# The stores' DMAs move from SyncE's queue to ScalarE's

## The chip, the cores and the metric

The kernel runs on one core of a Trainium2 chip. The metric is the device time of one execution in microseconds (us), the median of the runs shown. One execution was also taken with the hardware profiler; the rows below are of that one.

## The reference

The reference runs two blocks in a row on a sequence of 1024 tokens with 1024 features. The first block has two layers. Each layer mixes a grouped-query attention over the sequence and 256 context tokens, a windowed pooling and a neighbourhood attention on a grid of 64 columns; the context is updated in the first layer only.

```python
def first_block(x, c, ctx, ...):
    for l in range(2):
        h  = rms_norm(x, norm_gain[l]) * (1 + scale) + shift      # scale, shift, gate from silu(c) @ w_mod[l]
        hc = rms_norm(ctx, norm_gain[l]) * (1 + scale_c) + shift_c
        aq, ak, av, ag, bz, bg, nq, nk, nv, ng = split(h @ w_in[l])
        a_out = global_gqa(rope(norm(aq)), rope(norm(ak)), av, norm(ak_c), av_c)
        b_out = pool_branch(bz, pool_w[l], pool_scale[l])
        n_out = neighbourhood_attn(norm(nq), norm(nk), nv, norm(nk_c), nv_c, na_rpb[l])
        y = concat([a_out * silu(ag), b_out * silu(bg), n_out * silu(ng)]) @ w_out[l]
        x = x + gate * y
    return x

def second_block(x, p, ...):
    z = rmsnorm(x, g_mix) @ w_in
    y_fox  = fox_attention(q, k, v, log_f)               # causal, 8 heads, a decay as bias
    y_rwkv = rwkv7_scan(r, decay, k, v, -kk, kk * a)     # a recurrence over the 1024 tokens, 8 heads
    x = x + (sigmoid(gate_fox) * (y_fox @ w_o_fox) + sigmoid(gate_rwkv) * (y_rwkv @ w_o_rwkv)) @ w_out
    u = causal_dwconv(rmsnorm(x, g_ffn) @ w_up)
    x = x + (gelu(u[:, :2816]) * u[:, 2816:]) @ w_down
    return x + sigmoid(rmsnorm(x, g_ple) @ w_ple_gate) * (p @ w_ple_up)
```

## The kernel before

Activations lie with features on the 128 partitions and tokens along the free dimension. A product of full accuracy is made of three matmuls: each operand is split into a rounded part (`wh`, `h`; a cast on ScalarE, lines 271, 280 and 282) and the remainder (`wl`; a subtraction on VectorE, line 272). A weight tile comes by DMA into one of two raw buffers `wr` (line 290), is split, and the raw buffer is free again when the subtraction is done.

The stages follow each other in this order.

- **First block, twice** (`gqa`, `na`, `mix`). `gqa` projects queries, keys and values, takes the row maxima of the scores (`max_steps`) and then the exact softmax (`exact_steps`). One step of `exact_steps` makes, for each of two heads, a score bank `sp` on TensorE (two buffers) and its exponential `p` on ScalarE (line 694); the product with the values follows one step later. At the end of a pair of heads ScalarE copies the sum out (line 728), VectorE takes the reciprocal of the row sums (line 729), GpSimd multiplies (line 730), and the result `yr` is stored to the DRAM tensor `yd`. While the last attention units run, `na_project` makes the neighbourhood attention's queries, keys and values, 20 pieces of 128 tokens in each layer, and stores each piece to DRAM: `nv` to `nvd`, and the turned tiles `nt` to `nk1d`, `nk2d` and `nq1d` (lines 980 and 985). ScalarE or VectorE copies `nt` out of PSUM (lines 321 and 323). `na` loads them again, gates its result on GpSimd (line 1093) and stores it; beside it run the gates (`gate_steps`, a GpSimd product at line 950) and the pooling. `mix` loads all of `yd` (line 278, `h<-yd`) and the residual (line 1139, `x<-xd`), multiplies by `w_out` and adds in place (line 1148).
- **Second block**: `project` (projections, many stores of intermediates), `rwkv` (the recurrence as a chain of small matmuls with the causal attention woven in; its results are stored at line 1758 from `yc`, those of the attention from `yr`), `merge` (loads `yd` and, at line 1815, `x<-xd`), and `ffn` with 16 stores of the output at its end.

Every intermediate that goes through DRAM is written by one helper, `store` (lines 739 and 740). All loads, and the few stores that are not written with the helper, name SyncE's queue (SP) themselves.

What sets the order: the code is written in program order with two streams woven into each other (`weave`), but the framework's planner makes each engine's instruction stream from it. The planner keeps its own account of when operands and buffers are ready and puts the instruction that is ready and stands first in the program next. An engine, and the queue that it issues, then work strictly in that fixed order on the chip. An instruction waits for what it needs, and all that stands behind it on the same engine waits with it. A DMA instruction that SP issues thus stands in SP's stream, and one that ScalarE issues stands between ScalarE's activations and copies.

Of the kernel before, what the change touches and what calls it, by code (L numbers as in the profile page):

```python
# [216 lines left out]
class _Builder:  # L217
# [519 lines left out]
        return steps  # L737

    def store(self, dst, src):
        self.nc.sync.dma_start(out=dst, in_=src)  # L740

    def first_block(self):
        nc, tc, a = self.nc, self.tc, self.a
# [1212 lines left out]
```

## Time and profile before

| | |
|---|---|
| median of 3 runs | 4063.01 us (4056.43 to 4072.8) |
| profiled execution, its own time | 4071.35 us |
| its span, first to last instruction | 4069.6 us |
| mean granted TensorE clock | 0.955 |
| TensorE matmuls busy | 3755.1 us (92%) |
| VectorE / ScalarE / GpSimd busy | 2386.8 / 1612.1 / 929.7 us (59 / 40 / 23%) |
| DMA engines | 29.8% of 16 engines' span, all from one queue |

The profiled execution's own time is 1.75 us above its span and 8.3 us above the median of the runs. TensorE is the engine that the span follows; the rest of its time is spread over waits for other engines. DMA-issuing instructions are not counted as busy on any engine: on SP they are listed as SPq. A granted clock of 1.00 is full speed.

### The profile page before, as it was taken

Reading aid. Unit: us, or ns where it says so; the run is one execution under the profiler, and the core shown is the slowest. Engines: PE = TensorE matmul, PEld = TensorE weight load, DVE = VectorE, ACT = ScalarE, POOL = GpSimd, SP = SyncE. Lnnn points to the kernel's source line nnn. Section 1 sums busy time; section 2 is a strip of 40 time slices with the busy share of each in tenths; the row PEclk is TensorE's granted clock in tenths of the full one; section 3 lists DMA queues with packets and bytes.
Section 4 is the critical chain, followed back from the end, with each engine's and each line's share of the span. In section 5 each row is a group of like instructions: output and inputs, shape, how many; then the busy total and the mean of one; then the engine's idle time right before and its main releaser. Section 6 shows DMA issues by size and latency. Waiting matters only on the chain. (4 is left out here: it accounts for less than half of the span.)

```text
span 4069.6 us, 52648 instructions
## 1 busy us (share of the span) xinstructions
PE 3755.1 (92%) x18392; PEld 2809.5 (69%) x18392; DVE 2386.8 (59%) x5500; ACT 1612.1 (40%) x3251; POOL 929.7 (23%) x1127
## 2 busy tenths in 40 slices
PE   5899999888899999799999989989869999999999
PEld 4755666566755666478778866666648788888877
DVE  5888755645787747655664337776544543434354
ACT  4445663334346653543333234443343422222243
POOL 3233322311233324311110023343312100000020
PEclk8999999989999999899999978998879999999999
DMA  5111126564111135543333242121224411111133
GB/s 179 46 43 42 55 88 188 188 215 147 39 42 40 56 129 191 166 129 89 108 100 102 87 115 55 47 69 23 68 100 143 149 50 47 50 47 47 49 92 105
DMA packets 267890, 379.20 MB, mean 93 GB/s; under 512 B 56400, under 2 KB 145440, under 8 KB 264024
## 3 DMA queue, kind: packets, MB, share of 16 engines
q1 hardware_dynamic: 267624, 375.83, 29.8%
q8 instruction: 146, 2.39, 0.3%
q14 instruction: 120, 0.98, 0.1%
HBM read 280.90 MB, written 87.54 MB: 91 GB/s over the span
## 5 line engine op out<-in xcount | busy, mean ns | idle before, releaser
L223 PE MATMUL pp<-h,wh 128*128 128x512 f32 (+1 forms) x1696 | 527.3, 388 | 50.6 <-DVE x L1148 16.9
L223 PE MATMUL pp<-wh,h 128*128 128x384 f32 (+1 forms) x1792 | 518.2, 352 | 15.4 <-ACT v L548 12.6
L272 DVE TENSOR_TENSOR wl<-wr,wh 128x512 fp32r<-128x512 f32 (+3 forms) x386 | 299.7, 781 | 393.4 <-ACT wh L271 391.6
L223 PE MATMUL dd<-h,wh 128*128 128x512 f32 x1664 | 519.5, 393 | 0.0
L271 ACT CAST wh<-wr 128x512 fp32r<-128x512 f32 (+3 forms) x386 | 249.9, 651 | 611.3 <-PE pp L223 286.7
L223 PEld LDWEIGHTS pp<-h,wh 128*128 128x128 f32 x1696 | 315.7, 194 | 128.9 <-ACT wh L271 17.8
L709 POOL TENSOR_TENSOR acc<-acc,p 128x512 f32<-128x512 f32 (+3 forms) x246 | 295.3, 1200 | 443.3 <-ACT p L694 275.7
L223 PEld LDWEIGHTS dd<-h,wh 128*128 128x128 f32 x1664 | 312.5, 188 | 71.4 <-DVE h L478 0.3
L223 PEld LDWEIGHTS pp<-wh,h 128*128 128x128 f32 x1792 | 335.2, 194 | 34.0 <-ACT v L548 13.9
L223 PE MATMUL rp<-h,side 128*128 128x512 f32 x1440 | 350.6, 396 | 0.0
L223 PE MATMUL pp<-h,wl 128*128 128x512 f32 (+1 forms) x848 | 327.1, 386 | 1.0 <-DVE wl L272 0.9
L223 PE MATMUL dd<-h,wl 128*128 128x512 f32 x832 | 325.9, 392 | 0.0
L223 PE MATMUL pp<-wl,h 128*128 128x384 f32 (+1 forms) x896 | 312.6, 349 | 0.0
L223 PE MATMUL sp<-q,k 66*128 66x512 f32 (+6 forms) x944 | 300.1, 407 | 11.2 <-DVE p L692 5.7
L223 PEld LDWEIGHTS rp<-h,side 128*128 128x128 f32 x1440 | 266.5, 189 | 52.0
L634 DVE TENSOR_REDUCE mx<-mp 128x1 f32<-128x512 f32 (+1 forms) x472 | 250.7, 559 | 55.3 <-PE mp L223 53.4
L223 PE MATMUL mp<-k,q 128*128 128x512 f32 (+3 forms) x664 | 232.5, 383 | 13.5 <-DVE mx L634 6.4
L709 DVE TENSOR_TENSOR acc<-acc,p 128x512 f32<-128x512 f32 (+3 forms) x246 | 201.1, 817 | 68.0 <-ACT p L694 26.8
L223 PEld LDWEIGHTS sp<-q,k 128*128 128x128 f32 (+1 forms) x944 | 164.0, 192 | 108.7 <-issue 55.7
L694 ACT ACTIVATE p<-sp 128x512 f32<-128x512 f32 (+1 forms) x316 | 181.4, 594 | 141.3 <-PE sp L223 128.1
L223 PE MATMUL pp<-act,wh 128*128 128x512 f32 x704 | 221.4, 396 | 2.0 <-ACT act L271 1.1
L223 PE MATMUL vp<-p,v 128*64 128x512 f32 (+3 forms) x824 | 212.9, 596 | 5.5 <-ACT p L694 5.1
(371 smaller groups left out, 6705.5 us busy)
## 6 DMA issues: line engine op xcount, KB each, us to landing
wr<-in_w_out SPq DMA_DIRECT2D x96, 256.0 KB
wr<-in_w_up SPq DMA_DIRECT2D x88, 256.0 KB
wmod<-in_w_mod SPq DMA_DIRECT2D x16, 1024.0 KB
wr<-in_w_tok SPq DMA_DIRECT2D x40, 384.0 KB
xd<-x SPq DMA_DIRECT2D x6, 2048.0 KB
wr<-in_w_feat SPq DMA_DIRECT2D x40, 256.0 KB
bq<-in_na_bias SPq DMA_DIRECT2D x16, 640.0 KB
yd<-yr SPq DMA_DIRECT2D x32, 256.0 KB
```

The lines of the kernel that those rows point to most:

```text
L223: return self.nc.tensor.matmul(out, lhsT=lhsT, rhs=rhs, start=start, stop=stop)
L271: self.nc.scalar.copy(out=hi, in_=src)
L272: self.nc.vector.tensor_tensor(out=lo, in0=src, in1=hi.bitcast(F32), op=ALU.subtract)
L634: nc.vector.tensor_reduce(out=m, in_=ps[:, :n], axis=AX.X, op=ALU.max)
L694: made = nc.scalar.activation(out=p[:, j, :n], in_=st[:, :n], func=AF.Exp)
L709: u.summed = eng.tensor_tensor(out=u.acc[:, j, q0:q0 + n], in0=u.acc[:, j, q0:q0 + n], in1=p[:, j, :n], op=ALU.add)
```

## The change

The helper that writes every intermediate and the output issues its DMA on ScalarE's queue instead of SP's. All loads stay on SP, and so do the few transfers that do not go through the helper (queries from SBUF to SBUF, the two bounces of the recurrence through DRAM, and the row `crow`).

```diff
     def store(self, dst, src):
-        self.nc.sync.dma_start(out=dst, in_=src)
+        self.nc.scalar.dma_start(out=dst, in_=src)
```

## Rows read from the trace of the kernel before

**Rows 1.** The page: busy time, share of the span and instructions of each engine.
```profile
PE 3755.1 (92%) x18392; PEld 2809.5 (69%) x18392; DVE 2386.8 (59%) x5500; ACT 1612.1 (40%) x3251; POOL 929.7 (23%) x1127
```

**Rows 2.** Stretches: length, busy PE, PEld, DVE, ACT, POOL, clock, DMA share, GB/s.
```profile
350.00:600.00 250.00, 237.92 (x1148) 155.79 (x1147) 178.29 (x408) 153.27 (x325) 85.60 (x112) 1.00 0.19 55
...
1300.00:1500.00 200.00, 189.88 (x911) 127.98 (x911) 132.93 (x325) 130.09 (x271) 64.77 (x90) 1.00 0.21 63
...
1800.00:2400.00 600.00, 562.26 (x2765) 472.69 (x2765) 293.29 (x911) 188.29 (x481) 58.51 (x146) 0.97 0.34 104
```

**Rows 3.** Line 740, the store: count, issue in ns (least/median/most), first and last start.
```profile
L740 SPq DMA_DIRECT2D nvd<-nv x40: 327/331/566, 338.0 to 1482.8; - x40
L740 SPq DMA_DIRECT2D nk1d<-nt x40: 522/532/610, 370.3 to 1485.5; - x40
L740 SPq DMA_DIRECT2D nk2d<-nt x40: 838/857/928, 374.5 to 1486.7; - x40
...
L740 SPq DMA_DIRECT2D nq1d<-nt x36: 531/546/905, 375.5 to 1492.7; - x36
```

**Rows 4.** Waits of SP's queue: line, what it waited for, us in total, times, longest.
```profile
SPq L290 <- DVE wl L272: 1050.6, 303, 15.4
SPq L740 <- POOL yr L730: 136.4, 23, 23.4
...
SPq L740 <- DVE nt L323: 42.9, 24, 4.5
...
SPq L740 <- POOL yr L1093: 35.9, 9, 9.0
...
SPq L740 <- POOL kk L1406: 17.7, 7, 5.9
...
SPq L740 <- POOL gy L950: 15.3, 8, 4.2
```

**Rows 5.** Waits between TensorE and the exponentials, 350 to 600 us.
```profile
PEld vp L223 <- ACT p L694: 11.1, 30, 1.4
...
ACT p L694 <- PE sp L223: 26.2, 26, 2.0
```

**Rows 6.** Lines 729 and 730, between the copy of a result and its store.
```profile
L729 DVE RECIPROCAL yr<-sp x38: 1745/3358/3359, 165.1 to 2998.3; 128x512 f32<-128x512 f32 x32, 128x256 f32<-128x256 f32 x6
...
L730 POOL TENSOR_TENSOR yr<-yr x38: 727/1282/1722, 166.9 to 3001.8; 128x512 f32<-128x512 f32 x32, 128x256 f32<-128x256 f32 x6
```

**Rows 7.** Timeline around the end of `rwkv`: start, us, instruction [idle before <-releaser].
```profile
3003.11 0.33 SPq L740 DMA_DIRECT2D yd<-yr  x1
...
3008.44 0.32 SPq L740 DMA_DIRECT2D yd<-yc  x1
3008.85 0.39 SPq L1815 DMA_DIRECT2D x<-xd  x1
3010.70 0.37 SPq L278 DMA_DIRECT2D h<-yd  x1
...
3024.55 1.22 PE L223 MATMUL pp<-h,wh 128*128 128x512 f32 x2 [16.54 <-ACT wh L271]
```

**Rows 8.** Timeline at the end of the second `na`.
```profile
1665.09 29.87 SPq L290 DMA_DIRECT2D wr<-in_w_out  x5
1697.41 0.33 SPq L740 DMA_DIRECT2D yd<-yr  x1
...
1698.31 0.41 SPq L1139 DMA_DIRECT2D x<-xd  x1
...
1707.69 1.22 PE L223 MATMUL pp<-h,wh 128*128 128x512 f32 x2 [14.14 <-DVE x L1148]
```

**Rows 9.** Timeline inside `rwkv`, a result's store on SP and ScalarE's stream beside it.
```profile
2518.24 0.53 SPq L1322 DMA_DIRECT2D kk<-fk2d  x1
2528.70 0.34 SPq L740 DMA_DIRECT2D yd<-yr  x1
...
2527.22 0.58 ACT L1663 COPY tq<-c 128x512 f32<-128x512 f32 x1 [3.67 <-PE c L223]
```

## The prediction

> **What bounds the kernel now.** I read the page's busy line first. The reader is to see that TensorE's matmuls fill 92% of the span and ScalarE's own work only 40% [rows 1]: whatever costs TensorE no time costs nothing, and ScalarE has room on average. An average hides the stages, so the stretches come next [rows 2]. In the two stretches in which the softmax runs beside the neighbourhood projections (350 to 600 and 1300 to 1500 us) ScalarE is busy 153.27 of 250 and 130.09 of 200 us, 61% and 65%, and TensorE 95%. In `project` (1800 to 2400) ScalarE is busy 31%. Then the store line by itself, for what one issue holds a queue [rows 3], and the waits of SP's queue, for what stands ahead of what [rows 4]. The waits between TensorE and the exponentials tell how close these two engines run [rows 5]. Last come the timelines where TensorE stands longest, to see whether a load was late because a store stood ahead of it [rows 7, 8].
>
> **What the change removes from SP.** Nearly all loads of weights wait for their raw buffer, not for the queue: 1050.6 us of SP's waiting is for the subtraction that frees `wr` [rows 4]. Such a load does not start earlier when stores leave the queue. I cost this at nothing; the cover is that split weights lie several tiles ahead, and no wait of TensorE in the rows of the inner loops names a load.
>
> Stores do stand ahead of loads where a stage ends. At the end of `rwkv`, SP issues a store at 3003.11 and the next at 3008.44; the 2 MB residual load goes out at 3008.85, and the last load of `yd`, whose casts and products come last ahead of TensorE's first matmul after 16.54 us of idleness, only at 3010.70, behind those 2 MB [rows 7]. With the second store gone from SP the residual can go right after what is left of SP's work, at about 3005.6, so some 3.3 us earlier, and the last load of `yd` lands as much earlier. At the end of the second `na` SP is through with the loads ahead at 1694.96, then waits until 1697.41 for the store's operand, and issues the residual at 1698.31; TensorE waits 14.14 us for the chain behind it [rows 8]. Here the gain is 2.4 us. Together I take **6 us off**. Bounds: nothing, if the residual's buffer comes free no earlier than that; and 30.7 us, the two idle times whole, if it had been ready long before. I stay near the low end, because after the residual still come a load, two casts and a subtraction that do not change.
>
> By the Trainium skill, DMA: Bandwidth & Descriptors, section Issuing engines are not separate DMA queues, issuing from more than one engine saves only the sequencer's time for starting the DMA. By that rule the waiting ahead of these loads is no gain and the sum below would be 6 us higher; no row of the kernel before, where one queue issues all, decides it.
>
> **What it adds to ScalarE: the issues.** Of the stores of line 740 the four rows of the neighbourhood projections stand here; 15 more rows, 266 stores, are most of them like the row of `nvd` [rows 3]. Those of the projections hold a queue for 40 x 0.331 + 40 x 0.532 + 40 x 0.857 + 36 x 0.546 = 88.5 us, 156 instructions, nearly all inside the two stretches. There ScalarE goes from 283.4 to 371.9 of 450 us, from 63% to 83%, and each issue stands in order between the exponentials that TensorE waits for.
>
> How much of it reaches TensorE is read from the two sides of the softmax [rows 5]: TensorE's weight loads for the value products waited 30 times for an exponential, 0.37 us each, and ScalarE waited 26 times for the scores, 1.0 us each. So about half of the exponentials have no slack, the other half have about 1 us, which hides one issue. I charge half of the 156 stores with 0.37 us: **29 us**. Bounds: nothing, if the planner lays every issue into ScalarE's idle time; 88.5 us, if every one is passed on whole.
>
> The other stores have cover: over a third of them lie in `project`, where a bank of TensorE is filled by 24 matmuls and ScalarE is two thirds idle [rows 2]. I cost them at nothing; without that cover, at 0.33 us each, the 266 would be 88 us.
>
> **What it adds to ScalarE: the waits.** Where ScalarE itself made the operand, the store waits for work that ScalarE does anyway. Where GpSimd made it, ScalarE stands still until GpSimd is done, with every activation behind it. SP's waits for such operands are 136.4 + 35.9 + 17.7 + 15.3 = 205.3 us in 23 + 9 + 7 + 8 = 47 places [rows 4]. The longest chain is the one of a softmax result: after ScalarE's copy the reciprocal takes 3.36 us and GpSimd's product 1.28 us [rows 6]. One case stands in `rwkv` [rows 9]: SP has nothing to issue from 2518.77 to 2528.70; ScalarE stands idle for 3.67 us of it and has one copy at 2527.22 that TensorE's chain needs. A store that the planner puts ahead of this copy holds the chain for about 1.5 us, from 2527.22 to 2528.70; one that it puts behind, hardly.
>
> Since the planner goes by its own account, not by the chip, I take half of the 47 places as put too early, by one product of GpSimd, 1.28 us: **30 us**. Bounds: nothing, and all of the 205.3 us. I stay far below the upper end because SP waits with nothing else to do, while ScalarE reaches the same store later, with other work done ahead of it. Waits for VectorE's `nt` are 42.9 us on SP in 24 places [rows 4]; they fall on stores that are charged above, and I add nothing for them; 42.9 us is their bound.
>
> By the Trainium skill, Perfetto Trace Analysis, section Per-instruction lifecycle, an activation goes into a wait queue and leaves the sequencer free, while a DMA keeps the sequencer from its wait until its descriptors are made. By that rule these waits hold all of ScalarE's later work. No row of the kernel before shows a store in ScalarE's stream.
>
> For the clock I take nothing: the stretches with many short waits run at 1.00 [rows 2].
>
> **The sum.** 29 + 30 - 6 = 53 us on the profiled execution: its own time of 4071.35 becomes about 4124. That execution is 8.3 us above the median of the runs, 4063.01, so the forecast for a median is 4063 + 53 = **4116 us**. About 0.5% (20 us) is what a measurement of this kernel can tell from no change.
>
> **The rivals.**
>
> *ScalarE jams (slower than forecast).* If the planner's account of GpSimd and of the reciprocal is short in most places, the 205.3 us of waits move onto ScalarE, and the 88.5 us of issues pass on too. Half of the two, 147 us, gives 4210. For it: the three engines' chain is long [rows 6], and 83% in order leaves little room. Against it: outside the two stretches ScalarE is busy 1612.1 - 283.4 = 1328.7 of about 3620 us, 37% [rows 1, 2].
>
> *No change.* The planner sees ScalarE's idle 37% in the stretches and puts stores there and behind work that is ready. Charges of a third of mine, 20 us, less the 6 us, give 4077, within 20 us of before. For it: ScalarE's idle time before an exponential is 1.0 us and most issues are 0.33 to 0.55 us [rows 3, 5]. Against it: the issue of `nk2d`, 0.86 us, and the two beside it come within a few us of each other in each piece.
>
> *Faster.* The loads at the ends of the stages are what counts. If the residual loads were ready 10 us or more before SP came to them, each of the two idle times [rows 7, 8] shrinks by that, some 22 us together, the charges on ScalarE stay in its idle time, and the time is 4041. It decides from about 10 us of earlier issue at each; the case for it is that SP did stand waiting for a store in both places, the case against it that only 3.3 and 2.4 us of that waiting is seen right ahead of the residuals.
>
> *The change does not do what it says:* the planner could order the rest of SP's stream so that loads wait as before, which is again no change in time; it is in that rival's chance.
>
> **How the numbers follow.** The forecast, slower by 20 to 100 us, has 0.50; the jam, above 100 us, 0.17; no change 0.22; faster by over 20 us 0.11. Slower by over 0.5% is then 0.50 + 0.17 = 0.67. The range: below 4042 lies about half of the faster case, 0.06; above 4200 a good half of the jam, 0.10. So 4042 to 4200 holds the time in about 8 of 10; the likeliest case's own range is 4083 to 4163.
>
> **What would show it.** The waits of TensorE for the exponentials in the two stretches grow from 11.1 us to some 25 us each; a step that passes nothing on would leave them. Waits of ScalarE's sequencer at line 740 for GpSimd's `yr` appear, of 1 to 3 us. TensorE's 16.54 us at the end of `rwkv` and 14.14 us at the second `mix` shrink by about 3 and 2 us; the wait of line 290 for `wl` stays near 1050 us. `project` and everything after 3100 us last as long as before. I am wrong if TensorE's busy time per stretch is unchanged in the two softmax stretches while the total moves, or if TensorE begins to wait for ScalarE in `project`.

## The result and the profile after

The changed kernel takes 4084.41 us (median of 10 runs, 4073.84 to 4098.92) against 4066.05 us for the kernel before in the same rounds (10 runs): ratio 1.0052, 95% interval 1.0034 to 1.0071, so about 21 us slower (14 to 29 by the interval; the two medians by themselves are 18 us apart, and some expectations below say +18). The forecast was 53 us slower. The direction was right, the size was not.

The profiled execution's own time is 4086.5 us, its span 4084.6 us. The page's busy line, which answers [rows 1]:

```profile
PE 3757.1 (92%) x18392; PEld 2811.5 (69%) x18392; DVE 2391.2 (59%) x5500; ACT 1614.7 (40%) x3253; POOL 925.6 (23%) x1127
```

The same work stands in it; TensorE needs 2 us more for it. The stretches of [rows 2] after the change, in the same columns:

```profile
350.00:600.00 250.00, 237.51 (x1122) 154.73 (x1121) 176.27 (x404) 152.08 (x323) 84.62 (x113) 0.99 0.18 51
1300.00:1500.00 200.00, 193.07 (x932) 131.04 (x931) 140.81 (x341) 132.07 (x273) 65.36 (x89) 0.99 0.17 51
1800.00:2400.00 600.00, 569.24 (x2812) 479.71 (x2812) 298.74 (x908) 187.37 (x478) 59.84 (x144) 0.98 0.32 102
```

TensorE is as busy as before in the first softmax stretch (237.51 for 237.92) and busier in the second and in `project`. The later two windows do not hold quite the same work, since all of it has slid back by some 20 to 30 us. By the starts of equal matmuls in the two traces the changed kernel loses 4 us in the first stretch and wins 3 us in the second. By the prediction's own test ("wrong if TensorE's busy time per stretch is unchanged in the two softmax stretches while the total moves") its account of where the loss sits is thus wrong. By the same starts it is 29 us late at the end of the first block (1720 us), 5 us late in `merge` (3030 us) and 15 us late at the end: the first block and the feed-forward part lose, and `project` and `rwkv` win back most of it. (The profiled execution of before is itself 8 us longer than the mean of its runs.) Line 740, which answers [rows 3] (ns least/median/most, first and last start):

```profile
L740 ACTq DMA_DIRECT2D nvd<-nv x40: 326/330/624, 337.4 to 1502.5; - x40
L740 ACTq DMA_DIRECT2D nk1d<-nt x40: 520/531/1383, 373.9 to 1505.3; - x40
L740 ACTq DMA_DIRECT2D nk2d<-nt x40: 857/865/1421, 376.5 to 1506.8; - x40
...
L740 ACTq DMA_DIRECT2D nq1d<-nt x36: 527/533/559, 378.6 to 1512.5; - x36
```

The issues hold ScalarE as long as they held SP: 40 x 0.330 + 40 x 0.531 + 40 x 0.865 + 36 x 0.533 = 88.2 us. But the waits of TensorE for the exponentials from 350 to 600 us went down, where 11.1 us [rows 5] were to become some 25 (us, times, longest):

```profile
ACT p L694 <- PE sp L223: 21.9, 18, 2.2
...
PEld vp L223 <- ACT p L694: 7.0, 21, 1.1
```

A mere insertion of stores can't do that. The planner lays all streams anew when 430 DMAs change their engine: in the built programs 2809 of TensorE's 16000 instructions follow another instruction than before, and 994 of ScalarE's 3069 when the stores between them are left out.

### The profile page after: what moved, and what is told of

Read it like the earlier page. It is cut to its first block, busy times and chain, and to the rows that moved or that the text cites. A ratio compares the mean times of both kernels' runs of the same rounds, so it can differ in the third digit from the quotient of the medians.

```text
span 4084.6 us, 52421 instructions
## 1 busy us (share of the span) xinstructions
PE 3757.1 (92%) x18392; PEld 2811.5 (69%) x18392; DVE 2391.2 (59%) x5500; ACT 1614.7 (40%) x3253; POOL 925.6 (23%) x1127
## 5 line engine op out<-in xcount | busy, mean ns | idle before, releaser
L223 PE MATMUL pp<-wh,h 128*128 128x384 f32 (+1 forms) x1792 | 508.7, 349 | 20.0 <-ACT v L548 17.6
```

The costliest lines, as they stand in the source:

```text
L223: return self.nc.tensor.matmul(out, lhsT=lhsT, rhs=rhs, start=start, stop=stop)
```

## Experiments

Three theories were held against each other. Theory 1 is the prediction's: half of the issues and half of the waits on ScalarE reach TensorE. Theory 2: the issues fall into slack; the loss comes from waiting for operands that GpSimd makes (for the first two runs with a fixed order it was written down more strictly: neither costs anything). Theory 3: the new order, not the stores, makes the time. A time below is the ratio to the kernel before in the same rounds, less one, times 4064 us; 95% intervals in brackets.

**Parts of the change, with the planner's own order for each.** The helper is split, and only some call sites use the new one:

```
+    def store_act(self, dst, src): self.nc.scalar.dma_start(out=dst, in_=src)
 ...
-                        self.store(self.nd[dst][pr, :, :, r], t)
+                        self.store_act(self.nd[dst][pr, :, :, r], t)
```

> Only the 156 stores of the neighbourhood projections go from ScalarE; the other stores stay on SyncE. Theory 1 (the prediction's: half of their issues hold TensorE by 0.37 us each): +29 us against the kernel before. Theory 2 (the issues fall into slack of ScalarE and TensorE's order; the loss comes from operands that GpSimd makes): -5 to +6 us. Theory 3 (any edit makes the planner lay all streams anew, and that alone moves the time): anywhere within 20 us of before, and this run, the run with the GpSimd-made stores alone and the run with the rest do not add up to +18.

> Only the stores whose operand GpSimd has made (the attention results, the gated products, kk) go from ScalarE; the others stay on SyncE. Theory 1: half of the places by 1.28 us, less the earlier loads at two stage ends: +30 - 6 = +24 us. Theory 2: this part carries most of the change's +18: +10 to +20 us, and ScalarE stands some 1.3 to 1.5 us at each of these stores. Theory 3: anywhere within 20 us of before.

> All stores go from ScalarE except those of the neighbourhood projections and those whose operand GpSimd has made. Theory 1: 0 us (these were costed at nothing). Theory 2: -5 to +5 us. Theory 3: anywhere within 20 us of before.

Measured: ratio 1.0031 [1.0018, 1.0043], +13 us; 1.0042 [1.0028, 1.0057], +17 us; 1.0077 [1.0061, 1.0093], +31 us. The sum is 61 us, three times what all stores together cost, and the part that theory 1 priced at nothing and theory 2 at 5 us at most is the dearest; its 31 us are also more than the 20 us that theory 3 allowed. Parts that don't add up speak for theory 3: each run has an order of its own.

**The waits without a DMA, planner's order.**

```
-        self.nc.sync.dma_start(out=dst, in_=src)
+        self.nc.sync.dma_start(out=dst, in_=src); self.look(src)
+    def look(self, src): n = len(src.shape) - 1; self.nc.scalar.copy(out=self.scratch[n][:src.shape[0]], in_=src[(slice(None),) + (slice(0, 1),) * n])
```

> All stores stay on SyncE as in the kernel before; beside each of the stores of the helper ScalarE copies one element per partition of the stored operand into a scratch tile, so ScalarE waits for the same operands as in the changed kernel and works a fraction of a microsecond on each, with no DMA in its stream. Theory 1 and theory 2 (what costs is ScalarE standing for operands made elsewhere): +10 to +30 us. The rival that the loss comes from two queues sharing completion semaphores, so that loads wait for stores to land: within 5 us of before. Theory 3: anywhere within 20 us.

Measured: 1.0128 [1.0111, 1.0145], +52 us. More than any theory allowed, and by the starts of equal instructions in the two traces over 30 us of it appear at one place, between 700 and 850 us. Theories 1 and 2 would spread it over all stores. The run could not tell order from copies, so the order had to be held fixed.

**The order held fixed.** The next kernels contain, as data, the order that the planner gave to another kernel, and tie each instruction to the one ahead of it on its engine with an edge of issue order that waits for nothing:

```
+    for k in np.cumsum(...ORDER...):
+        name = "I-%d" % k
+        if name in found and name not in pre:
+            e = str(found[name].engine)
+            if e in last:
+                tc.add_manual_dep(found[name], last[e], edge)
+            last[e] = name
```

Here `edge` is the kind of edge without a wait, and the "..." stand for the unpacking of the data. Only the moved (or added) instructions are left for the planner to place. The edges themselves cost nothing that can be seen: a run below that has them, and 156 small copies besides, is within 5 us of before. This gives two factors, order and place of the stores, that vary apart.

> All stores go from ScalarE as in the changed kernel, but every other instruction of all five engines keeps the order that the planner gave it in the kernel before (edges of issue order, no waits); only where a store stands in ScalarE's stream is the planner's. What is left is the stores' own cost on ScalarE and the gain on SyncE. Theory 1 (half of issues and waits reach TensorE, in the order of before): +53 us. Theory 2 (issues and waits fall into slack): -6 to +6 us against before. Theory 3 (the time is in the new order that the planner makes, not in the stores): -6 to +6 us too, and the run with the new order and no moved store then shows the change's +18.

> No store is moved, all go from SyncE as before, but every other instruction of all engines stands in the order that the planner gave it in the changed kernel. Theory 3 (the new order alone costs): +12 to +25 us against before. Theories 1 and 2 (the stores in ScalarE's stream cost, by issue, by waits, or by loads bound to their landings): -5 to +5 us.

| stores from | order of before | order of the changed kernel |
|---|---|---|
| SyncE | 0 (the kernel before) | 1.0020 [1.0010, 1.0030], +8 us |
| ScalarE | 1.0099 [1.0086, 1.0112], +40 us | 1.0052 [1.0034, 1.0071], +21 us (the change) |

Theory 1 had +53 for the lower left, theories 2 and 3 about nothing. With the order kept, the stores cost 40 us. In the order that the planner makes once it knows of them they cost 21 - 8 = 13 us, and that order costs 8 us by itself. So new planning gives back 19 us net, and both theory 2 and theory 3 in their pure form fall. (The 8 us, 4 to 12 by the interval, lie between the two expectations.) The row of the exponentials, 350 to 600 us, in the changed kernel's order with all stores on SyncE:

```profile
PEld vp L223 <- ACT p L694: 4.2, 16, 0.4
```

The moved stores raise it in this order too, from 4.2 to the 7.0 us shown above, but the order by itself lowers it from 11.1 to 4.2.

**The parts with the order of before.**

> Only the 156 stores of the neighbourhood projections go from ScalarE, all other instructions in the order of before. Theory 1: +29 us. Theories 2 and 3: -3 to +5 us (the same 156 stores with the planner's own order cost +13).

> Only the stores of operands that GpSimd has made go from ScalarE, all other instructions in the order of before. Theory 1: +30 - 6 = +24 us. Theory 2: +10 to +18 us. Theory 3: -6 to +5 us (the same stores with the planner's own order cost +17).

> All stores go from ScalarE except those of the neighbourhood projections and those of operands that GpSimd has made; all other instructions in the order of before. If the costs of the parts add up in a fixed order (all stores +40, projections +19 to +22, GpSimd's +10): +5 to +12 us. The rival that a part of the +40 comes only with all stores on the second queue (loads on SyncE bound to landings of stores on ScalarE's): -3 to +3 us. The prediction: 0.

Measured: 1.0055 [1.0043, 1.0068], +22 us; 1.0030 [1.0018, 1.0043], +12 us; 1.0030 [1.0019, 1.0040], +12 us. Now the parts add up within their intervals: 46 us against 40 for all. GpSimd's 12 lie in theory 2's range and the rest's 12 in that for costs that add up. TensorE's weight loads in the first run, 350 to 610 us, to be held against [rows 5]:

```profile
PEld vp L223 <- ACT p L694: 15.7, 35, 1.2
...
PEld sp L223 <- ACT p L694: 6.0, 11, 1.2
```

The prediction's mark, exponentials that come later, is there as soon as nothing else moves: 11.1 us have become 15.7, a third of the rise to 25 that was forecast, and the second row has grown from 2.4. By the starts of equal matmuls 16 us of loss arise in the two softmax stretches of this run.

**Issue time or waiting?** One kernel issues each of the 156 stores of the projections a second time, into DRAM that nobody reads; two others leave all stores on SyncE and give ScalarE a copy of one element per partition that waits for what the store would wait for.

The first pair of lines is against the run with these stores on ScalarE, the second against the kernel before; each shows one of two places.

```
-  self.store_act(self.nd[dst][pr, :, :, r], t)
+  self.store_act(self.nd[dst][pr, :, :, r], t); self.again(self.nn[dst][pr, :, :, r], t)      # pin_double
-  self.store(self.nd[dst][pr, :, :, r], t)
+  self.store(self.nd[dst][pr, :, :, r], t); self.look(t)                                     # pin_wait
```

> As the run with the 156 stores of the projections on ScalarE in the order of before (+19 to +22 us), but each of them is issued twice, the second time into a DRAM tile that nobody reads. The second issue adds issue time (some 88 us in all) and no wait. If the issue time is what reaches TensorE: +35 to +45 us against before. If the waits for the operands are: +18 to +26 us.

> No store is moved and all instructions stand in the order of before; beside each of the 156 stores of the projections ScalarE copies one element per partition of the stored operand into a scratch tile, so it waits for the operands as in the run with these stores on ScalarE, with some 0.2 us of work each (about 31 us in all) in place of the issue. If the issue time is what reaches TensorE: +4 to +9 us. If the waits are: +15 to +22 us.

> No store is moved and all instructions stand in the order of before; beside each of the 66 stores of operands that GpSimd has made ScalarE has a copy of one element per partition (about 0.2 us) that waits for GpSimd's product and has no DMA. If the +12 us of these stores on ScalarE is ScalarE's waiting for GpSimd (the prediction's 30 us): +8 to +14 us. If it is their issue time (66 issues, some 22 us): -2 to +4 us.

Measured: 1.0215 [1.0202, 1.0228], +87 us; 1.0002 [0.9992, 1.0012], +1 us; 1.0012 [0.9999, 1.0024], +5 us. The first 88 us of issues cost 22 us, a quarter; the second 88 us cost 87 - 22 = 65 us, three quarters: the first use up slack. The +87 is more than twice what either expectation had. (The doubled stores also write twice the bytes; the row below names the exponentials, not the transfers.) TensorE's weight loads with the doubled issues, 350 to 650 us, and then with the waits alone, 350 to 600 us:

```profile
PEld vp L223 <- ACT p L694: 29.2, 33, 3.9
PEld sp L223 <- ACT p L694: 14.3, 12, 3.4
```

```profile
PEld vp L223 <- ACT p L694: 9.9, 29, 1.4
...
PEld sp L223 <- ACT p L694: 3.3, 10, 0.7
```

With the waits alone the first row is 9.9 us, no more than the 11.1 of before. ScalarE does stand: the same 350 to 600 us of that run show its copies waiting for `nt`,

```profile
ACT scratch L741 <- DVE nt L323: 10.4, 8, 4.5
```

but the kernel is no slower by it (-3 to +5 us). For the projections it is the issue time that costs. A rival, that loads on SyncE come late because they wait for landings of these stores (last section), is not seen there: in the two stretches no wait of TensorE or its weight loads is for a DMA, neither before nor in the run with these stores on ScalarE. For GpSimd's operands the waits alone cost 5 us (0 to 10) of the 12, between the two expectations; the two intervals overlap, so how those 12 divide stays open.

**Is an order alone worth tens of us?**

> No store is moved and no copy is added: the kernel before, in the order that the planner made for the run with a copy beside every store (+52 us). If that run's loss is the order's: +35 to +50 us. If it is the copies themselves, or ScalarE's waiting for the operands: -5 to +10 us.

> No store is moved. The first block and the feed-forward part keep the order of before; project, rwkv and merge stand in the order that the planner made for the changed kernel. If what the new order gains there is the order's own (TensorE's idle time fell by some 3 + 7 + 4 us in the three stages of the run with the new order, the stages got 33 us shorter in that profile): -12 to -30 us against before, faster than both kernels. If the shorter stages were the granted clock's drift from run to run: -5 to +5 us.

The first is the kernel before in the order of the run with copies: 1.0111 [1.0098, 1.0124], +45 us of that run's 52, with no copy and no moved store. TensorE's waits from 690 to 850 us in it (in the kernel before the wait of the first row, over the same stretch, is 4.5 us, 4 times):

```profile
PE tp L223 <- DVE zw L1026: 20.5, 6, 4.7
PE mp L223 <- DVE mx L636: 7.5, 12, 1.0
PE mp L223 <- DMA modrow<-in_w_mod: 3.7, 2, 2.6
```

In that order TensorE stands at the pooling's matmuls until VectorE has `zw`, 3.4 us each time. The second kernel joins two orders, one chain of edges for each of the three parts: 0.9923 [0.9910, 0.9936], 31 us faster than before and 51 us faster than the changed kernel, 4032.98 us. It contains no part of the change, only the order that the change brought about from `project` to `merge`. Laid against before by the starts of equal instructions, TensorE's idle time is shorter by 3 us in `project`, 11 in `rwkv` and 4 in `merge`; the rest is a shorter busy time late in `rwkv`, at a higher granted clock. The last stretch of `rwkv` in it and then in the kernel before, columns as in [rows 2]:

```profile
2790.00:2980.00 190.00, 156.85 (x1104) 117.26 (x1102) 123.28 (x364) 75.47 (x173) 62.63 (x66) 0.86 0.21 56
```

```profile
2800.00:3008.00 208.00, 173.36 (x1129) 128.10 (x1127) 123.15 (x357) 73.15 (x164) 63.88 (x68) 0.80 0.16 43
```

The mean granted clock is 0.86 for 0.80 of full speed. Part of that is the one profile's: over the matmuls that before runs from 2800 to 2900 us its own profile shows 0.83 and TensorE busy for 89.2 us, while the seven other profiles with the order of before show 0.90 or 0.91 and 80.8 to 83.4 us. In the next 105 us of work the clock does go with the order: 0.75 to 0.80 in all eight profiles with the order of before, 0.82 or 0.83 in the three with the new one (the changed kernel, the one in its order with the stores on SyncE, and this one). What in the order raised it no run here shows.

## Why the prediction was wrong

**The step that failed: the sum took the order of all other instructions for unchanged and gave the new one no term.** The prediction said itself that the planner makes the streams, but its sum laid the issues and waits into the streams of before and took TensorE's loss there as the change's. For that kernel it came close: 53 forecast, 40 measured in the order of before; in part by luck, since a term that is too large and a missing one nearly cancel (below). The planner's new order then took back 19 of the 40, and the changed kernel is at 21.

The order's own 8 us are the difference of larger amounts. By the starts of equal matmuls the kernel with the new order and all stores on SyncE is 19 us late at the end of the first block (1720 us), 14 us early in `merge` (3030 us), and 5 us early at the end, after the feed-forward part. (Against the profiled run of before; the 8 us are from many runs of each.) With the order of before and the stores on ScalarE the kernel is 32 us late at 1720 us, 33 at 3030 us and 32 at the end. One place where the new order loses can be read from 600 to 790 us, where TensorE before waited 4.0 us in all. After the change, from 600 to 800 us:

```profile
PE sp L223 <- DMA q<-nmt: 5.8, 1, 5.8
PE mp L223 <- DMA modrow<-in_w_mod: 2.9, 4, 1.5
PE mp L223 <- DVE mx L636: 2.4, 1, 2.4
PE mp L223 <- DVE zw L1025: 1.6, 1, 1.6
```

And with the changed kernel's order but all stores on SyncE, from 590 to 790 us:

```profile
PE mp L223 <- DVE mx L634: 4.7, 1, 4.7
PE mp L223 <- DMA modrow<-in_w_mod: 2.7, 4, 1.6
PE sp L223 <- DMA q<-nmt: 2.5, 1, 2.5
PE mp L223 <- DVE zw L1025: 2.3, 1, 2.3
```

Nearly the same late operands, with no store moved. The feed-forward part loses too, which the prediction had as unchanged after 3100 us. Timeline of VectorE there after the change, and the row of before that answers to it:

```profile
3218.95 0.69 DVE L448 TENSOR_TENSOR nrb<-nrb,y 128x512 f32<-128x512 f32 x1
3226.31 0.16 DVE L249 TENSOR_SCALAR rsv<-vp 128x4 f32<-128x4 f32 x1 [6.68 <-PE vp L223]
```

```profile
3213.03 0.69 DVE L448 TENSOR_TENSOR nrb<-nrb,y 128x512 f32<-128x512 f32 x1
3214.93 0.16 DVE L249 TENSOR_SCALAR rsv<-vp 128x4 f32<-128x4 f32 x1 [1.21 <-PE vp L223]
```

VectorE's sum of squares is ready in both, but TensorE's reduction of it now stands behind other matmuls, and every operand of the next matmuls comes 5.5 us later. TensorE's lateness grows from 5 to 15 us between 3215 and 3250: it stands for 5.5 us in three gaps, and behind them the granted clock is 0.69 from 3231 to 3242 us and 0.80 from 3250 to 3256 us, while in the kernel before it is 1.00 over the matmuls that answer to these. The kernel in the new order with the stores on SyncE loses 8 us there.

**Term by term, in the order of before.**
- *Issues of the projections, 29 us:* about right. 22 measured (17 to 28), by the mechanism named (later exponentials); doubling the issues makes the same rows grow.
- *Other stores, 0 us:* wrong by the 12 us of the 208 stores of the rest; the term also held the 66 of GpSimd's operands. Their cover was read from `project`, where the run with the rest alone indeed shows none of it (after the change, too, TensorE waits for ScalarE there only 5.1 us, before 3.6); in that run by the starts of equal instructions, 6 of the us are lost between 1500 and 1720, in the gates and the end of the second `na`, a stretch that the prediction did not look at. (They are 274 stores, not 266: 430 were moved in all.)
- *Waits for GpSimd, 30 us:* mis-sized, and for 66 stores rather than the 47 places at which SP had waited. ScalarE did stand as foreseen; after the change the case of [rows 9] reads, in the timeline of ScalarE,

```profile
2542.80 0.33 ACTq L740 DMA_DIRECT2D yd<-yr  x1
2543.17 0.59 ACT L1670 COPY tq<-c 128x512 f32<-128x512 f32 x1 [3.14 <-POOL yr L730]
```

  3.14 us for `yr`, just above the 1 to 3 us forecast. But TensorE, 2541.53 to 2545, stood only 1.08 us, and for an operand of VectorE. The whole of these stores costs 12 us, of which the waits are 0 to 10. The rule cited from the Trainium skill (Perfetto Trace Analysis, section Per-instruction lifecycle), that a DMA holds the sequencer from its wait until its descriptors are made, agrees with this row: the copy starts when the issue is over. That ScalarE's standing is TensorE's loss was the prediction's addition; the runs with waits alone show 5 us of it at most for the projections and 10 at most for GpSimd's operands.
- *Earlier residual loads, -6 us:* the idle times did shrink, 16.54 to 12.27 and 14.14 to 12.49, together about as forecast, but mostly not for that reason. With the order of before and the stores on ScalarE, TensorE's idle time is 15.84 us at the end of `rwkv` and 13.06 at the end of the second `na`, so 1.8 us of the 6 are the stores'; with the new order and the stores on SyncE it is 12.61 and 11.95. SP's queue at the end of `rwkv` in the first of these two kernels:

```profile
3038.79 0.36 SPq L278 DMA_DIRECT2D h<-yd  x1
3039.24 0.46 SPq L1815 DMA_DIRECT2D x<-xd  x1
3047.62 0.36 SPq L278 DMA_DIRECT2D h<-yd  x1
```

  The residual goes out 2.8 us ahead of the store of `yc` (ScalarE issues it at 3042.03) instead of 0.4 us behind it, a gain of 3.2 us as worked out. But its 2 MB are then ahead of that store: the load that waits for the store goes out 5.6 us behind it, before 2.3 [rows 7]. What was won at the issue was lost in the transfer. In the changed kernel's order the residual comes last, at 3022.22, and the 4 us are there with the stores on either queue. By the rule that the prediction took from the Trainium skill (DMA: Bandwidth & Descriptors, section Issuing engines are not separate DMA queues), that issuing from more than one engine saves only the sequencer's time for starting the DMA, there was to be no gain; the run with the order of before agrees within 0.7 us here and 1.1 at `na`.
- *L290 for `wl` near 1050 us:* missed; 1190.8 us now, 319 times, and 1051.5 with the new order and the stores on SyncE. SP, rid of the stores, stands longer for the buffers. That fits the forecast that such loads do not start earlier, but their starts were not compared.
- *The luck in the sum:* for GpSimd's operands 18 us too much were forecast, for the rest 12 too little.

Of the rivals *the planner reorders* was named, but only as a way to no change and without a price; it should have had a term of its own with either sign.

## What to carry to other kernels

Where a planner makes the streams, a change of an engine is two changes: the cost in the old order, and a new order, which in the three kernels that had it alone was worth -31, +8 and +45 us with the same instructions. Hold the order fixed to measure the first, and test the order with nothing else changed to measure the second; a version that looks like an effect of the edit may be an order that can be had without it. A DMA issued from a busy engine costs issue time on that engine; here a quarter of the first 88 us reached the kernel's time and three quarters of the next 88.

## What the runs showed of the hardware that was not expected

SP's loads of weights now wait for landings of stores that the other queue issued; before, no row of line 290 names a store. SP's waits after the change:

```profile
SPq L290 <- DMA nk2d<-nt: 105.6, 2, 58.1
```

The load has no data in common with that store. In the built program the DMAs of both queues tell of their landing on the same eight semaphores, and such a load waits for one of them. With the order of before and all stores on ScalarE the like wait is 112.1 us, 3 times, for `nk1d`. TensorE hardly feels it there: its waits for a DMA are 10.3 us in the whole run against 11.5 before, and those for parts of split weights (`wh`, `wl`) 16.8 against 18.1.
